# Stores issued from ScalarE's queue, attention outputs of two heads in turn, and three more cache buffers

## The chip, the cores and the metric

One NeuronCore of one Trainium2 chip runs the whole kernel. The metric is device time in microseconds of one execution, taken as the median of several runs.

The engines that matter here are TensorE (PE: matmuls, and PEld for its weight loads), VectorE (DVE), ScalarE (ACT), GpSimd (POOL) and SyncE (SP). SP only issues DMAs here. Each engine takes its instructions in the order in which the program lists them, and a DMA is one instruction on the engine that issues it.

## What is computed

The kernel runs one layer of a streaming encoder for 1024 prompt frames (8 tiles of 128) and 128 decode frames (8 requests of 16; a ninth tile, number 8). The reference, cut to the parts that this change touches:

```python
qa, ka, va, fl, qb, kb, vb, ga, gb = split(rms_norm(h, g_mix) @ w_in)   # 8 + 8 heads of 64
log_f = log_sigmoid(fl + b_f)
# outputs beside y: normalised ka, va, log_f of every frame, kb, vb of the newest 512 frames and the decode frames
s = q @ k.T * 64**-0.5 + bias        # mixer A: forget sums, causal; mixer B: relative bias, own chunk + 8 before
y = softmax(s) @ v                   # decode: keys/values are the cache (2048 rows A, 512 rows B) and the new ones
h += (sigmoid(ga) * (ya @ w_up_a) + sigmoid(gb) * (yb @ w_up_b)) @ w_out
h += peer_ffn(rms_norm(h))           # 8 heads x top-16 of 128*128 experts: rows of u and v per frame
h += sigmoid(rms_norm(h) @ w_ple_gate) * (p @ w_ple_proj)
```

## The kernel before

**Two groups of tiles.** Group 0 holds the decode tile and prompt tiles 0 to 2, group 1 the prompt tiles 3 to 7. By the profile's time the stages are: norm and attention of group 0 with the decode attention (0 to 510 us; "stage 0" below), its merge (510 to 715), its routing with the norm and first projections of group 1 ("route 0", 715 to 905), attention of group 1 ("attention 1", 905 to 1390), merge (1390 to 1710), routing ("route 1", 1710 to 2021), the expansion of group 1's expert weights into dense matrices G ("expand", 2021 to 2305), the dense expert pass (2305 to 3925) and the per-layer embedding (3925 to 4084).

**Attention** goes by units: a unit is two heads of one mixer, 64 columns each, side by side in one 128-wide tile. `project` makes q, k, v of one unit and tile, stores k and v to the outputs (L328, L329) and, in group 0, also the transposed keys and the values to the DRAM scratch `kT_d`, `v_d` (L350, L351), from which group 1 reads them back. `prompt` works one tile of one unit: for each of its two heads the scores `N`, the softmax `p`, transposes of `p` into `pt` (L494), an evacuation to SBUF as `pT` by ACT (`evac`, L80), and the output matmuls `po` (L497), whose two heads fill PSUM partitions 0 to 63 and 64 to 127, that is columns 0 to 63 and 64 to 127 of the array. Its score matmul for mixer A adds the forget sums with a selector `sel_p`.

**Decode** (group 0 only) streams the cache: keys `kcd` (L522) and values `vcd` (L586) come in pieces of 128 x 512 (256 KB) through one ring of `KC` buffers. A phase of four requests loads 16 key pieces (mixer A), makes the scores `Sd` (L547), the softmax, the transposes, and then the outputs `pod` (L591). These use four column groups of 32 in turn, one request in each. The code is interleaved: a unit's projections alternate with the attention of the unit before.

**Expert rows.** Group 0's experts are fetched row by row: an indirect DMA from POOL (L813) into a ring of 4, then one DVE instruction (L816 for u, L818 for v). There are 1,024 of these steps. They have low priority: a scheduler lays the first `G0` = 400 of them between the instructions of group 1 up to expand, by its own estimate of when each engine is free. Group 1's expand builds G (`ga`, `pg`, `stage`, L919 to L929) and stores it in 10 pieces of 4 MB (`G_d`, L933); some hidden units are worked out ahead and stored as `ge_d` (L968).

**Queues.** All loads and all stores are issued from SP, except the gathers. DMAs of SP and ACT take the semaphores DMAHW0 to DMAHW7 in turn, and an issue waits until the DMA that had the same semaphore before it has landed.

Of the kernel before, what the change touches and what calls it, by code (L numbers as in the profile page):

```python
# [8 lines left out]
F32 = mybir.dt.float32  # L9
F32R = mybir.dt.float32r  # L10
# [8 lines left out]
P = 128  # L19
# [7 lines left out]
PRE = tuple(range(3, 128, 4)) + tuple(range(1, 128, 32))  # L27
KC = 15
NP = 4
# [17 lines left out]
def build(tc, I, O, dbg=None, stop=None):  # L47
# [46 lines left out]
    m_blk = [const.tile([P, P], BF, name=f"m_blk{s}") for s in range(2)]  # L94
    sel_p = const.tile([P, 8, P], F32R, name="sel_p")
    qn = const.tile([P, 2], F32, name="qn")
# [33 lines left out]
    def setup_masks(dec):  # L130
# [18 lines left out]
        for s in range(2):  # L149
# [12 lines left out]
            nc.vector.tensor_copy(m_new[s], a)  # L162
        for q in range(2):
            t1 = tmp(f"t1{q}").rearrange("p (h c) -> p h c", h=4)
            t2 = tmp(f"t2{q}").rearrange("p (h c) -> p h c", h=4)

            o3 = one.rearrange("p (h c) -> p h c", h=4)
            for t, off in ((t1, 4 * q), (t2, 32 + 4 * q)):
                keep(t, o3, [[-1, 4], [0, P]], 0.0, -off, 1)
                keep(t, t, [[1, 4], [0, P]], 0.0, off, -1)  # L170
            nc.vector.tensor_tensor(sel_p[:, 4 * q:4 * q + 4, :], t1, t2, op=OP.add)
        for q in range(2):
# [87 lines left out]
    def attention_phase(g, tiles, aT, yT):  # L260
# [17 lines left out]
        def load_unit(u):  # L278
# [12 lines left out]
            if br == 1:  # L291
                Dn = at.tile([P, 2, 256], F32, tag="Dn", name=f"Dn{g}{u}")
                nc.sync.dma_start(Dn, I["biasP"][u - 4])
                for h in range(2):
                    hh = 2 * (u - 4) + h
                    nc.vector.tensor_scalar(Dn[:, h, :], Dn[:, h, :], rb0[:, hh:hh + 1], -1.0,
                                            op0=OP.subtract, op1=OP.mult)
                    nc.vector.memset(Dn[0:64, h, 192:256], BIG)
            return ws, kT, vU, Dn

        def project(u, n, t, ws, kT, vU, Dn):
# [25 lines left out]
            if ko is not None:  # L327
                nc.sync.dma_start(ko[rows, cu * P:(cu + 1) * P], kq[:, 0:P])  # L328
                nc.sync.dma_start(vo[rows, cu * P:(cu + 1) * P], vt)  # L329
            tp = bank(f"tp{nm}")  # L330
            nc.tensor.transpose(tp[:, 0:P], kq[:, 0:P], ident)
            nc.tensor.transpose(tp[:, P:2 * P], kq[:, P:2 * P], ident)
            qp = at.tile([P, 2, P], F32, tag="qp", name=f"qp{nm}", bufs=2 * nts if g == 0 else nts + 1)
            nc.gpsimd.memset(qp, 0.0)
            if t == TS:
                kTs = at.tile([P, P], F32, tag="kTs", name=f"kTs{nm}")
                nc.scalar.copy(kTs, tp[:, 0:P])
                q4 = qp.rearrange("p a c -> p (a c)").rearrange("p (b h i) -> p b h i", b=8, h=2)
                for h in range(2):
                    s = slice(64 * h, 64 * h + 64)  # L340
                    nc.scalar.activation(q4[s, :, h, :], tp[s, P:2 * P].rearrange("p (b i) -> p b i", i=16),
                                         AF.Copy, scale=qn[s, br:br + 1])
                pending.append(decode(u, br, qp, kTs, vU[:, slot[TS], :], n, at, dec, yT))
            else:
                nc.scalar.copy(kT[:, t * P:(t + 1) * P], tp[:, 0:P])
                for h in range(2):
                    s = slice(64 * h, 64 * h + 64)
                    nc.scalar.activation(qp[s, h, :], tp[s, P:2 * P], AF.Copy, scale=qn[s, br:br + 1])
                if g < len(GROUPS) - 1:
                    nc.sync.dma_start(kT_d[u, :, t * P:(t + 1) * P], kT[:, t * P:(t + 1) * P])  # L350
                    nc.sync.dma_start(v_d[u, :, t, :], vt)  # L351
                pending.append([lambda: prompt(g, u, br, t, n, qp, kT, vU, Dn, at, yT)])
# [27 lines left out]
    def logf(g, tiles, fl, at, dec):  # L380
# [31 lines left out]
        for i, t in enumerate(tiles):  # L412
            nc.sync.dma_start(O["lf"][:, t * P:(t + 1) * P], lT[0:8, i, :])
        pt = [t for t in tiles if t != TS]
# [37 lines left out]
    def prompt(g, u, br, t, n, qp, kT, vU, Dn, at, yT):  # L452
# [3 lines left out]
        W = nk * P  # L456
        po = bank(f"po{nm}")
        both = W <= 512 and wide[0] == 1024
        for h in range(2):
# [3 lines left out]
            for c0 in range(0, W, 512):  # L463
# [3 lines left out]
                if br == 0:  # L467
                    nc.tensor.matmul(N[:, c0:c1], qp[:, h, :], rhs, start=True, stop=False)
                    nc.tensor.matmul(N[:, c0:c1], sel_p[:, 2 * u + h, :], cP[:, c0:c1], start=False, stop=not last)
                    if last:  # L470
# [19 lines left out]
            for j0 in range(0, nk, 4):  # L490
# [4 lines left out]
                evac(pT[:, j0:j1, :], ps[:, 0:(j1 - j0) * P].rearrange("p (j c) -> p j c", c=P))  # L495
            for j in range(nk):
                nc.tensor.matmul(po[64 * h:64 * h + 64, 0:P], vU[:, k0 + j, 64 * h:64 * h + 64], pT[:, j, :],  # L497
                                 start=j == 0, stop=j == nk - 1)
        nc.scalar.copy(yT[:, u, n * P:(n + 1) * P], po[:, 0:P])
# [385 lines left out]
    def expand_phase():  # L885
# [21 lines left out]
        for n, t in enumerate(DT):  # L907
            rb, gT = ready
            for c0 in range(0, P, W):
# [22 lines left out]
                if c0 % 64 == 64 - W:  # L932
                    nc.sync.dma_start(G_d[2 * n + c0 // 64], stage)  # L933
        st.close()
# [28 lines left out]
    def hidden_phase(dn, n2h, n2l):  # L963
        with tc.high_priority(offset=FILL):
            for q, j in enumerate(PRE):
                ge = dn.tile([P, TD], F32, tag="ge", name=f"gp{j}")
                hidden(dn, ge, j, n2h, n2l, nc.gpsimd, True)
                nc.sync.dma_start(ge_d[q], ge)  # L968

# [221 lines left out]
```

## Time and profile before

| | us |
|---|---|
| three runs | 4101.39, 4101.27, 4084.70 |
| median | 4101.27 |
| the profiled execution | 4085.47 |
| its span, first to last instruction | 4083.8 |
| PE, DVE, ACT, POOL busy in it | 3716.3, 2969.9, 1539.4, 1721.3 |

The profiled execution is at the lower of the two levels of the three runs. The granted TensorE clock over the span is 0.964 of full speed. PE is busy for 91% of the span, but not in each stage for the same reason, so the profile has to be read by stages: busy time of each engine in the stage, then the waits of the busiest, then the mean of one instruction times its count.

### The profile page before, as it was taken

The page shows a single profiled execution, that of the slowest core. Times are in us where ns is not written, and L with a number is a line of the kernel's source. Part 1 is how long each engine was busy: PE and PEld are TensorE (multiplying, and loading weights), DVE is VectorE, ACT ScalarE, POOL GpSimd, SP SyncE. Part 2 cuts the span into 40 slices and gives each one's busy share as a digit, 9 for nine tenths or more (in the row PEclk, how much of TensorE's full clock was granted, in tenths as well). Part 3 has the DMA queues.
Part 4 walks back from the last instruction along what each step waited for, and adds up shares of the span by engine and source line. Part 5 has one row for each costly group of instructions (what it writes and reads, how often), then busy time and mean ns, then how long its engine had stood idle before and what let it go on. Part 6 is the DMA issues. An engine that isn't in the chain of part 4 may idle for free.

```text
span 4083.8 us, 57125 instructions
## 1 busy us (share of the span) xinstructions
PE 3716.3 (91%) x20520; PEld 3048.3 (75%) x20520; DVE 2969.9 (73%) x5571; ACT 1539.4 (38%) x3307; POOL 1721.3 (42%) x1360
## 2 busy tenths in 40 slices
PE   7988899869889897899897899999999999999999
PEld 6555566657767565798886788888888888888876
DVE  5122112899888777799888588888888888888862
ACT  5445412346565411224599722222222222212231
POOL 5112032137767555652310044555555555555520
PEclk8999999879999898899999999999999999999999
DMA  6777733328888898972343589989988998988952
GB/s 206 237 235 208 223 93 124 101 82 268 281 288 275 286 321 294 328 247 88 108 184 165 230 297 314 325 309 315 325 304 304 313 331 316 327 298 311 313 173 71
DMA packets 415116, 1002.49 MB, mean 245 GB/s; under 512 B 38816, under 2 KB 170352, under 8 KB 412400
## 3 DMA queue, kind: packets, MB, share of 16 engines
q0 software_dynamic: 147456, 536.94, 38.0%
q1 hardware_dynamic: 267376, 461.90, 34.0%
q8 instruction: 161, 2.64, 0.3%
q14 instruction: 123, 1.01, 0.1%
HBM read 917.19 MB, written 81.50 MB: 245 GB/s over the span
## 4 chain that ended last, share of the span: by engine, by line
issue 25%; PE 22%; DMA 20%; DVE 19%; POOL 11%; ACT 3%; SPq 0%; POOLq 0%; DVEq 0%; ACTq 0%
DMA v<-in_pv,gi 9%; POOL u L813 6%; DMA u<-in_pu,gi 5%; POOL v L813 4%; DVE gya L818 3%; DVE u L816 3%; PE Sd L547 2%; DMA vs<-in_pv 1%; DMA vcd<-in_vA 1%; PE z L209 1%; PE pu L638 1%; PE hd L958 1%; PE po L497 1%; PE z L210 1%; PE z L211 1%
## 5 line engine op out<-in xcount | busy, mean ns | idle before, releaser
L813 POOL DMA_INDIRECT v<-in_pv,gi x512 | 669.5, 1308 | 794.0 <-DVE gya L818 654.9
L813 POOL DMA_INDIRECT u<-in_pu,gi x512 | 669.2, 1307 | 494.3 <-DVE u L816 374.4
L816 DVE SCALAR_TENSOR_TENSOR u<-u,gn 128x1024 f32<-128x1024 f32 x512 | 630.0, 1239 | 167.0 <-DMA u<-in_pu,gi 164.5
L818 DVE SCALAR_TENSOR_TENSOR gya<-v,hid,gya 128x1024 f32<-128x1024 f32 x512 | 661.1, 1291 | 121.3 <-DMA v<-in_pv,gi 117.4
L1009 PE MATMUL py<-vh,wh 128*128 128x512 f32 x1280 | 507.9, 398 | 46.4 <-DVE yacc L1012 23.0
L1011 PE MATMUL py<-vh,wl 128*128 128x512 f32 x1280 | 497.9, 394 | 6.4 <-DVE wl L941 6.4
L1010 PE MATMUL py<-vl,wh 128*128 128x512 f32 x1280 | 502.4, 394 | 0.2 <-DVE vl L941 0.2
L958 PE MATMUL hd<-aTh,uh 128*128 128x320 f32 x2048 | 483.4, 313 | 21.0 <-ACT gp L961 14.1
L958 PE MATMUL hd<-aTh,ul 128*128 128x320 f32 x2048 | 482.8, 313 | 7.0 <-DVE ul L941 5.7
L958 PE MATMUL hd<-aTl,uh 128*128 128x320 f32 x2048 | 482.0, 313 | 0.0
L958 PEld LDWEIGHTS hd<-aTh,uh 128*128 128x128 f32 x2048 | 351.8, 191 | 31.9 <-ACT gp L961 16.0
L958 PEld LDWEIGHTS hd<-aTh,ul 128*128 128x128 f32 x2048 | 349.9, 190 | 13.7 <-DVE ul L941 7.8
L958 PEld LDWEIGHTS hd<-aTl,uh 128*128 128x128 f32 x2048 | 351.1, 191 | 4.0
L940 ACT CAST vh<-vs 128x1024 fp32r<-128x1024 f32 x128 | 134.1, 1052 | 500.0 <-DMA vs<-in_pv 267.7
L1009 PEld LDWEIGHTS py<-vh,wh 128*128 128x128 f32 x1280 | 242.4, 190 | 106.9 <-DVE yacc L1012 29.4
L1011 PEld LDWEIGHTS py<-vh,wl 128*128 128x128 f32 x1280 | 242.4, 189 | 61.3 <-DVE wl L941 10.6
L1010 PEld LDWEIGHTS py<-vl,wh 128*128 128x128 f32 x1280 | 242.8, 190 | 47.5 <-DVE vl L941 0.4
L940 ACT CAST uh<-us 128x1024 fp32r<-128x1024 f32 x128 | 134.2, 1048 | 285.7 <-PE hd L958 266.7
L940 ACT CAST wh<-ge 128x640 fp32r<-128x640 f32 x128 | 91.9, 727 | 390.7 <-DVE ge L987 195.5
L927 PE MATMUL pg<-obb,ga 128*128 128x128 f32 x1280 | 192.5, 296 | 42.2 <-ACT ga L923 22.2
L927 PEld LDWEIGHTS pg<-obb,ga 128*128 128x128 f32 x1280 | 164.0, 195 | 70.5 <-ACT ga L923 28.8
L1012 DVE TENSOR_TENSOR yacc<-yacc,py 128x1024 f32<-128x1024 f32 x160 | 192.4, 1214 | 11.5 <-PE py L1011 11.5
(1051 smaller groups left out, 7368.7 us busy)
## 6 DMA issues: line engine op xcount, KB each, us to landing
us<-in_uT SPq DMA_DIRECT2D x128, 512.0 KB
vs<-in_pv SPq DMA_DIRECT2D x128, 512.0 KB
G_d<-stage SPq DMA_DIRECT2D x10, 4096.0 KB
gj<-G_d SPq DMA_DIRECT2D x64, 640.0 KB
kcd<-in_kA SPq DMA_DIRECT2D x128, 256.0 KB
vcd<-in_vA SPq DMA_DIRECT2D x128, 256.0 KB
ge_d<-gp SPq DMA_DIRECT2D x36, 320.0 KB
ge<-ge_d SPq DMA_DIRECT2D x36, 320.0 KB
```

What stands on the lines that cost most here:

```text
L209: nc.tensor.matmul(out, lh[:, k, :], wh[:, a:b], start=first and k == 0, stop=False)
L547: nc.tensor.matmul(ps[32 * b4:32 * b4 + 32, :], q3[:, 4 * s + b4, :], rhs, start=br == 1 and q < nch, stop=True)
L813: nc.gpsimd.indirect_dma_start(out=r, out_offset=None, in_=I["pu" if k < P else "pv"], in_offset=bass.IndirectOffsetOnAxis(ap=gi[:, kk:kk ...
L816: nc.vector.scalar_tensor_tensor(r, r, 1.0, n2, op0=OP.mult, op1=OP.mult, accum_out=hid[:, kk:kk + 1])
L818: nc.vector.scalar_tensor_tensor(ya, r, hid[:, kk:kk + 1], ya, op0=OP.mult, op1=OP.add)
L927: nc.tensor.matmul(pg[:, c * P:(c + 1) * P], ga[:, b0 + c, :], ob[:, b0 + c, :], start=True, stop=True)
L940: nc.scalar.copy(out_h, src)
L958: nc.tensor.matmul(ps[sp][:, 0:Nw], a[:, k, :], b[:, k, sp * Nw:(sp + 1) * Nw], start=k == 0 and q == 0, stop=k == 7 and q == 2)
L1009: nc.tensor.matmul(py[:, c], wh[:, ns], vh[:, c], start=a, stop=False)
L1010: nc.tensor.matmul(py[:, c], wh[:, ns], vl[:, c], start=False, stop=False)
L1011: nc.tensor.matmul(py[:, c], wl[:, ns], vh[:, c], start=False, stop=z)
L1012: nc.vector.tensor_tensor(yacc[n], yacc[n], py, op=OP.add)
```

## The change

Three things change.

1. The stores of keys, values, log forgets, `kT_d`, `v_d`, `G_d` and `ge_d` are issued with `nc.scalar.dma_start` in place of `nc.sync.dma_start`, 215 DMAs in all (56 + 56 of values and keys, 24 + 24 to the scratch, 9 of log forgets, 10 of `G_d`, 36 of `ge_d`). A key store stands now behind the copy of the transposed keys.
2. In `prompt` both heads' `pT` are made first. Then `po` is allocated, and its matmuls alternate between the two heads, and so between the two column halves.
3. The selector `sel_p` shrinks from 8 x 128 to 8 columns (a broadcast supplies the rest), `qp` of group 0 has 6 buffers in place of 8, `Dn` one in place of two, and the cache ring `KC` 18 in place of 15.

```diff
-KC = 15
+KC = 18
...
-    sel_p = const.tile([P, 8, P], F32R, name="sel_p")
+    sel_p = const.tile([P, 8], F32R, name="sel_p")
...
-                Dn = at.tile([P, 2, 256], F32, tag="Dn", name=f"Dn{g}{u}")
+                Dn = at.tile([P, 2, 256], F32, tag="Dn", name=f"Dn{g}{u}", bufs=1)
...
             if ko is not None:
-                nc.sync.dma_start(ko[rows, cu * P:(cu + 1) * P], kq[:, 0:P])
-                nc.sync.dma_start(vo[rows, cu * P:(cu + 1) * P], vt)
+                nc.scalar.dma_start(vo[rows, cu * P:(cu + 1) * P], vt)
...
-            qp = at.tile([P, 2, P], F32, tag="qp", name=f"qp{nm}", bufs=2 * nts if g == 0 else nts + 1)
+            qp = at.tile([P, 2, P], F32, tag="qp", name=f"qp{nm}", bufs=nts + 2 if g == 0 else nts + 1)
...
                 nc.scalar.copy(kTs, tp[:, 0:P])
+                nc.scalar.dma_start(ko[rows, cu * P:(cu + 1) * P], kq[:, 0:P])
...
                 nc.scalar.copy(kT[:, t * P:(t + 1) * P], tp[:, 0:P])
+                if ko is not None:
+                    nc.scalar.dma_start(ko[rows, cu * P:(cu + 1) * P], kq[:, 0:P])
...
-                    nc.sync.dma_start(kT_d[u, :, t * P:(t + 1) * P], kT[:, t * P:(t + 1) * P])
-                    nc.sync.dma_start(v_d[u, :, t, :], vt)
+                    nc.scalar.dma_start(kT_d[u, :, t * P:(t + 1) * P], kT[:, t * P:(t + 1) * P])
+                    nc.scalar.dma_start(v_d[u, :, t, :], vt)
...
-            nc.sync.dma_start(O["lf"][:, t * P:(t + 1) * P], lT[0:8, i, :])
+            nc.scalar.dma_start(O["lf"][:, t * P:(t + 1) * P], lT[0:8, i, :])
...
-        po = bank(f"po{nm}")
+        pTs = []
...
-                    nc.tensor.matmul(N[:, c0:c1], sel_p[:, 2 * u + h, :], cP[:, c0:c1], start=False, stop=not last)
+                    nc.tensor.matmul(N[:, c0:c1], sel_p[:, 2 * u + h:2 * u + h + 1].broadcast_to([P, P]), cP[:, c0:c1], start=False, stop=not last)
...
-            for j in range(nk):
-                nc.tensor.matmul(po[64 * h:64 * h + 64, 0:P], vU[:, k0 + j, 64 * h:64 * h + 64], pT[:, j, :],
-                                 start=j == 0, stop=j == nk - 1)
+            pTs.append(pT)
+        po = bank(f"po{nm}")
+        for j in range(nk):
+            for h, pT in enumerate(pTs):
+                r = slice(64 * h, 64 * h + 64)
+                nc.tensor.matmul(po[r, 0:P], vU[:, k0 + j, r], pT[:, j, :], start=j == 0, stop=j == nk - 1)
...
-                    nc.sync.dma_start(G_d[2 * n + c0 // 64], stage)
+                    nc.scalar.dma_start(G_d[2 * n + c0 // 64], stage)
...
-                nc.sync.dma_start(ge_d[q], ge)
+                nc.scalar.dma_start(ge_d[q], ge)
```

**On TensorE, attention 1**, one pair of heads with 7 key tiles, before:

```order
L494 MATMUL pt_10859<-ident,p_10853 128x128 x4
L494 MATMUL pt_10865<-ident,p_10853 128x128 x3
L497 MATMUL po_10844<-pT_10858,vU_9920 64x128 x7
L494 MATMUL pt_10891<-ident,p_10885 128x128 x4
L474 MATMUL N_11103<-kT_10483,qp_10533 128x512
L494 MATMUL pt_10897<-ident,p_10885 128x128 x3
L497 MATMUL po_10844<-pT_10890,vU_9920 64x128 x7
```

and now (`po` is L501 there):

```order
L494 MATMUL pt_10876<-ident,p_10870 128x128 x4
L494 MATMUL pt_10882<-ident,p_10870 128x128 x3
L474 MATMUL N_11095<-kT_10476,qp_10526 128x512
L501 MATMUL po_10887<-pT_10850,vU_9913 64x128
L501 MATMUL po_10887<-pT_10875,vU_9913 64x128
```

Twelve more rows follow that repeat the last two. The two runs of seven have become one run of fourteen that alternates between the two `pT`, and no `pt` transposes stand between them any more.

**On SP, stage 0**, before, a key store stands among the loads of cache keys, with the waits in brackets:

```order
L522 DMA kcd_1223<-in_kA 128x512 [waits DMAHW1_49,PE_49]
L522 DMA kcd_1225<-in_kA 128x512 [waits DMAHW2_49,PE_49]
L328 DMA out_kA<-kq_1184 128x128 [waits DMAHW3_49,DVE_49,Activation_49]
L522 DMA kcd_1227<-in_kA 128x512 [waits DMAHW4_49,PE_49]
L522 DMA kcd_1229<-in_kA 128x512 [waits DMAHW5_49,PE_49]
L522 DMA kcd_1231<-in_kA 128x512 [waits DMAHW6_49,DMAHW2_49,PE_49]
L522 DMA kcd_1233<-in_kA 128x512 [waits DMAHW7_49,PE_49]
```

Now SP has loads alone, here at a later unit:

```order
L525 DMA kcd_4459<-in_kA 128x512 [waits DMAHW3_49,PE_49]
L525 DMA kcd_4461<-in_kA 128x512 [waits DMAHW4_49,PE_49]
L525 DMA kcd_4463<-in_kA 128x512 [waits DMAHW5_49,PE_49]
L525 DMA kcd_4465<-in_kA 128x512 [waits DMAHW6_49,PE_49]
L525 DMA kcd_4467<-in_kA 128x512 [waits DMAHW7_49,PE_49]
L525 DMA kcd_4469<-in_kA 128x512 [waits DMAHW0_49,PE_49]
L525 DMA kcd_4471<-in_kA 128x512 [waits DMAHW1_49,PE_49]
```

and ACT has the stores of that unit among its own work:

```order
L316 COPY vU_3919<-z_4111 128x128 [waits DVE_49]
L449 ACTIVATE p_4164<-p_4164,sm_4165 128x256 [waits DVE_49]
L345 DMA out_kA<-kq_4136 128x128 [waits DMAHW4_49,DVE_49]
L326 DMA out_vA<-vU_3919 128x128 [waits DMAHW6_49,Activation_49]
L351 DMA v_d<-vU_3919 128x128 [waits DMAHW0_49]
L502 COPY yT_253<-po_4075 128x128 [waits PE_49]
L447 ACTIVATE p_4178,sm_4179<-N_4174,mn_4176 128x256 [waits DVE_49]
L310 ACTIVATE kq_4264,ssz_4265<-z_4239 128x64 x4
L343 COPY kT_3918<-tp_4149 128x128 [waits PE_49]
```

The stores have moved from ahead of cache loads to ahead of ACT's copies. The semaphores that the three stores wait for (4, 6, 0) are those of three of the loads.

**On DVE, route 1**, from the last split of a weight (`wq17l`) on, where `tops`, `topi`, `sc` belong to the routing of group 1, and `gya` and `u` are expert rows of group 0; before:

```order
L701 TENSOR_TENSOR wq17l<-wq17s,wq17h 128x1024
L731 MAX tops_14841<-sc_15080 128x8 x2
L728 MAX tops_14838<-sc_15167 128x8 x2
L729 MAX_INDEX topi_14847<-tops_14842,sc_15094 128x8 x2
L821 TENSOR_TENSOR hid_8592<-hid_8592,gg_7593 128x128
L732 MAX_INDEX topi_14846<-tops_14841,sc_15080 128x8 x2
L729 MAX_INDEX topi_14843<-tops_14838,sc_15167 128x8 x2
L730 MATCH_REPLACE sc_15094<-tops_14842,sc_15094 128x128 x2
L818 SCALAR_TENSOR_TENSOR gya_8590<-v_0_8979,hid_8592,gya_8590 128x1024
```

and now (L819 is L816 of before, and L821 is L818):

```order
L704 TENSOR_TENSOR wq17l<-wq17s,wq17h 128x1024
L731 MAX tops_14831<-sc_15160 128x8 x2
L734 MAX tops_14834<-sc_15073 128x8 x2
L732 MAX_INDEX topi_14840<-tops_14835,sc_15087 128x8
L819 SCALAR_TENSOR_TENSOR u_113_8925,hid_8585<-u_113_8925,gn_8581 128x1024
L732 MAX_INDEX topi_14840<-tops_14835,sc_15087 128x8
L819 SCALAR_TENSOR_TENSOR u_114_8928,hid_8585<-u_114_8928,gn_8581 128x1024
L732 MAX_INDEX topi_14836<-tops_14831,sc_15160 128x8 x2
L819 SCALAR_TENSOR_TENSOR u_115_8931,hid_8585<-u_115_8931,gn_8581 128x1024
```

Here 16 expert-row steps stood between `wq17l` and the first `oa` of expand, and 31 stand there now. Ahead of the last attention instruction on DVE stood 219 of the 400, and now 206. Between this and `wq17l` the count is nearly as before.

## Rows read from the trace of the kernel before

**Rows 1.** Windows by stage: busy time (instructions) of each engine, TensorE clock, DMA share, GB/s.

```profile
core 0: us, PE busy (x) PEld busy (x) DVE busy (x) ACT busy (x) POOL busy (x), PEclk, DMA share, GB/s
0.00:510.00 510.00, 439.06 (x3406) 292.84 (x3406) 145.49 (x392) 253.07 (x838) 117.03 (x154) 0.94 0.74 222
...
905.00:1390.00 485.00, 432.27 (x2494) 335.64 (x2492) 414.19 (x783) 295.71 (x839) 344.18 (x294) 0.97 0.84 277
1390.00:1710.00 320.00, 273.66 (x1014) 192.99 (x1015) 242.91 (x341) 58.17 (x80) 185.87 (x145) 0.90 0.89 316
1710.00:2021.00 311.00, 286.87 (x1806) 276.95 (x1805) 294.28 (x1251) 111.84 (x193) 120.31 (x71) 0.96 0.50 166
2021.00:2305.00 284.00, 241.40 (x1632) 212.85 (x1630) 229.67 (x195) 283.25 (x502) 18.98 (x6) 0.98 0.39 159
2305.00:3925.00 1620.00, 1557.84 (x8256) 1378.14 (x8256) 1375.53 (x1517) 379.54 (x537) 835.31 (x621) 0.99 0.90 312
```

**Rows 2.** Groups of instructions, stage 0 (0:510): busy, mean ns, idle before and its releaser.

```profile
L591 PE MATMUL pod<-vcd,pTd 128*32 128x128 f32 x1280 | 54.1, 290 | 27.9 <-DMA vcd<-in_vA 26.6 <-ACT pTd L80 1.1
...
L497 PE MATMUL po<-pT,vU 128*64 128x128 f32 x192 | 33.2, 298 | 8.2 <-ACT pT L80 7.6
```

**Rows 3.** The same view, attention 1 (905:1390).

```profile
L816 DVE SCALAR_TENSOR_TENSOR u<-u,gn 128x1024 f32<-128x1024 f32 x128 | 160.9, 1262 | 28.0 <-DMA u<-in_pu,gi 27.2 <-DVE kq125r L216 0.4 <-issue 0.2
...
L497 PE MATMUL po<-pT,vU 128*64 128x128 f32 x856 | 118.1, 287 | 26.5 <-ACT pT L80 25.2 <-issue 1.2
...
L818 DVE SCALAR_TENSOR_TENSOR gya<-v,hid,gya 128x1024 f32<-128x1024 f32 x96 | 123.1, 1282 | 29.9 <-DMA v<-in_pv,gi 29.1 <-DVE gya L818 0.2 <-issue 0.2
```

**Rows 4.** Timeline of TensorE, 1113.5:1118: start, length, instruction and how many merged.

```profile
1114.34 1.09 PE L497 MATMUL po<-pT,vU 128*64 128x128 f32 x8
```

**Rows 5.** The chain that ended last, 0:510: start, length, what.

```profile
99.36 3.96 DMA kcd<-in_kA
...
155.28 1.29 PE pod L591 x34
157.11 9.32 DMA vcd<-in_vA
```

**Rows 6.** DVE's waits in attention 1 (905:1390): total, times, longest.

```profile
DVE gya L818 <- DMA v<-in_pv,gi: 29.1, 36, 2.1
DVE u L816 <- DMA u<-in_pu,gi: 27.2, 37, 2.0
```

**Rows 7.** Groups of instructions, route 1 (1710:2021).

```profile
L816 DVE SCALAR_TENSOR_TENSOR u<-u,gn 128x1024 f32<-128x1024 f32 x23 | 30.6, 1334 | 6.2 <-DMA u<-in_pu,gi 6.2
...
L818 DVE SCALAR_TENSOR_TENSOR gya<-v,hid,gya 128x1024 f32<-128x1024 f32 x16 | 25.2, 1573 | 0.0
```

**Rows 8.** Waits of SyncE's queue, stage 0 (0:510).

```profile
SPq L522 <- PE Sd L547: 50.6, 45, 5.0
...
SPq L328 <- DVE kq L316: 22.5, 10, 6.1
SPq L351 <- ACT vU L318: 13.8, 8, 4.0
SPq L350 <- ACT kT L345: 13.8, 12, 2.4
SPq L329 <- ACT vU L318: 13.1, 10, 2.0
...
SPq L586 <- DMA vcd<-in_vA: 9.9, 14, 1.7
```

**Rows 9.** TensorE's waits, stage 0 (0:510).

```profile
PE pod L591 <- DMA vcd<-in_vA: 26.6, 26, 2.5
PE z L209 <- ACT vU L318: 13.8, 3, 10.0
...
PE po L497 <- ACT pT L80: 7.6, 7, 1.4
PE ydd L596 <- ACT obd L594: 3.1, 6, 0.8
```

**Rows 10.** Issue of one line's DMAs: ns min/median/max, first and last start us.

```profile
L329 SPq DMA_DIRECT2D out_vA<-vU x16: 332/364/422, 64.6 to 400.7; - x16
```

**Rows 11.** Groups of instructions, expand (2021:2305).

```profile
L929 ACT COPY stage<-pg 128x512 f32<-128x512 f32 x158 | 151.9, 1153 | 0.7 <-PE pg L927 0.7
```

More of the change, by code (lines that the diff above doesn't have):

```diff
@@ L162, in setup_masks @@
             nc.vector.tensor_copy(m_new[s], a)
[L163 to L171, printed above, removed]
+        t1 = tmp("t1")[:, 0:8]
+        t2 = tmp("t2")[:, 0:8]
+        for t, off in ((t1, 0), (t2, 32)):
+            keep(t, one[:, 0:8], [[-1, 8]], 0.0, -off, 1)
+            keep(t, t, [[1, 8]], 0.0, off, -1)
+        nc.vector.tensor_tensor(sel_p, t1, t2, op=OP.add)
         for q in range(2):
```

## The prediction

> **What bounds the kernel now.** I read the table by stages first, then in each stage the waits of the engine that is busiest, and last the length of one instruction of each kind that the change touches. The stages have different limits [rows 1]. In stage 0 TensorE works 439 of 510 us and ScalarE only 253, so TensorE and what it waits for set the end. In attention 1 TensorE works 432 of 485 and VectorE 414, and VectorE also waits 29.1 + 27.2 = 56 us for expert rows to land [rows 6]: 414 + 56 = 470 of 485, so the row of expert-row steps is as near to the limit as TensorE is. There are 128 + 96 = 224 of these steps [rows 3], one each 485 / 224 = 2.17 us. In route 1 VectorE works 294 of 311, in expand ScalarE works 283 of 284, and in the dense pass TensorE works 1558 of 1620. The change adds nothing to the dense pass and takes nothing from it, so I leave it and the embedding at what they are.
>
> **Output matmuls on the two halves.** Before, eight `po` of one head start within 1.09 us less the last one's 0.29, so one each 0.11 us [rows 3, 4]. All eight use the same 64 columns. The nearest row with column groups in turn is the decode's `pod`, four groups of 32: 34 of them take 1.29 us, one each 0.03 us [rows 2, 5], though each moves 128 elements as `po` does. Four groups thus give nearly a factor of four, and two should give a factor of two: one `po` each 0.055 us. The saving of TensorE's time is 192 x 0.055 = 10 us in stage 0 [rows 2] and 856 x 0.055 = 47 us in attention 1 [rows 3]. The bounds are 0 and these. I take them whole as TensorE's time, since `pod` is the same form of instruction; what the stages make of it comes next.
>
> On this the Trainium skill ("TensorE: Matmul & The Clock Gate", section "Part 3: Packing small matmuls — row/col tiling") says that a weight load overlaps matmuls in flight only where its row group differs. Both halves use all 128 rows, so by that rule the loads would still queue and the saving be near 0; this is the fourth case below. The rule doesn't agree with the row of `pod`, whose four groups use all rows as well.
>
> **Attention 1 and route 1.** TensorE's 47 us don't all reach the end of the stage, since the expert rows pace it as well. The scheduler has put 206 of them ahead of the last attention instruction where 219 stood: 13 fewer, at 2.17 us, are 28 us. Between 0 (the stage is kept by something else) and 47 (TensorE alone sets it) I take 28, because VectorE was at 470 of 485. Its waits for projections and `pT` are small beside this. The 400 steps that precede expand are still 400. Merge 1 keeps its number, and route 1 gets 31 behind its last weight split where there were 16. In route 1 VectorE is the busy engine, and a step takes 1.33 us there [rows 7]: 15 x 1.33 = 20 us later into expand. The bounds are 3 (all of VectorE's 311 - 294 = 17 idle us taken up) and 15 x 1.57 = 24 [rows 7]. I take 20, since idle time there sits in front of results of TensorE and not where steps are. Attention 1 and route 1 together: -28 + 20 = -8, from -47 + 3 = -44 to +24.
>
> **Loads of the cache.** In stage 0 the stores' waits for data held up SP's queue 22.5 + 13.8 + 13.8 + 13.1 = 63 us [rows 8], and behind them stand the loads of keys and values. But SP waits as well for buffers, above all 50.6 us for `Sd` to release keys, and TensorE itself loses only 26.6 us to late values [rows 9]. Three more buffers let three more pieces be under way, and the lines of SP are free of stores. The gain lies between 0 and 26.6; pieces that TensorE waits for land 4 to 9 us after their issue [rows 5], and the longest wait is 2.5 us, so I take half, -13. The `qp` buffers, 8 to 6, and `Dn`, 2 to 1, cost nothing as long as `qp` is wanted for the tiles of one unit only; the expected cost is inside the bounds of the next term.
>
> On this the Trainium skill ("DMA: Bandwidth & Descriptors", section "Issuing engines are not separate DMA queues") says that all issuers share the same 16 engines, so that issuing from a second one saves the sequencer's issue time alone. By that rule the term would be 0 and the whole sum near -1. The rows show another thing that the move can save, the 63 us in which a store that waits for data stands ahead of loads; whether TensorE gets any of it no run here shows yet.
>
> **Stores on ScalarE.** 92 of the 215 stores fall into stage 0. One takes 0.33 to 0.36 us to issue [rows 10], so ScalarE gets 92 x 0.34 = 31 us of work. Beyond that a store waits for the DMA eight places earlier. In the order of the changed kernel that is, for some 70 of the 92, a load of SP. ScalarE then stands until that load has landed, and queued behind it are copies of `kT`, `vU`, `pT` and of `po`, for which TensorE waits. The nearest row is SP's own wait for the same thing, 9.9 us in 14 times, 0.7 each [rows 8]: 70 x 0.7 = 49 us. At the upper end half of a landing time of 4 us [rows 5] gives 70 x 2 = 140 us. How much of it reaches TensorE? Now 253 us of ScalarE's work [rows 1] cost TensorE 13.8 + 7.6 + 3.1 = 24.5 us of waits [rows 9], a tenth. A tenth of 31 + 49 to 31 + 140 is 8 to 17 us; I take +13. If it were a third of the upper end, it would be 57. In attention 1 some 77 stores add 77 x 0.34 = 26 us to ScalarE's 296 of 485; the loads ahead of them have long landed there, so a tenth of it, under 3 us, hides behind the pace of the expert rows. If that cover is gone it is the 3 us.
>
> **Expand.** ScalarE has no idle time there. Ten `G_d` issues are 10 x 0.36 = 3.6 us, and a few `ge_d` lie in it too: +4. If each issue also waits for the end of the copy before it, 1.15 us [rows 11], it is 4 + 11 = 15. That SP is relieved there brings nothing.
>
> **The sum.** Stage 0: -10 - 13 + 13 = -10. Attention 1 and route 1: -8. Expand: +4. Total -14 us on the profiled execution's 4085.5. That execution is at the lower of two levels of the three runs, 4085 and 4101. The median is at the upper one; I apply the sum to the median, 4101.3 - 14 = 4087.
>
> **The rivals.**
> - *B, the stages give TensorE's time back in full.* Attention 1 shrinks by 45 of its 47 us, because VectorE's 56 us of waits shrink too; route 1 takes up half of the moved steps in idle time, +10; of the late values 20 us vanish, and the stores cost stage 0 only +5, since ScalarE is idle for half of it. With -10 for `po` and +4 in expand that is -10 - 20 + 5 - 45 + 10 + 4 = -56: 4045. For it: both engines of attention 1 would fit into 440 us, TensorE with 385 and VectorE with 414 less 13 x 1.27. Against it: the pace of the expert rows would have to fall below 2.1 us.
> - *C, ScalarE's waits lengthen the decode.* A third of 171 us reaches TensorE, +57 in place of +13: the sum is +30, 4131. For it: ScalarE's copies stand right behind the stores in the order. Against it: ScalarE waits for TensorE much of the time, so some of the standing replaces a wait. It decides from the point at which stage 0 loses more than 13 + 14 = 27 us to it.
> - *D, the halves don't overlap* (the change doesn't do what it says). The -10 is gone. In attention 1 TensorE has its 432 us still, and of the 28 only half is left, while route 1 gets its 20: -13 + 13 - 14 + 20 + 4 = +10, 4111. Against it: `pod`.
>
> **How the numbers follow.** About 0.5%, 20 us, is what a measurement of this kernel can tell from no change: below 4081 is faster, above 4122 slower. The forecast of -14 has a chance of 0.41, B 0.34, C 0.17, D 0.08. Of the forecast's 0.41 some 0.08 fall below -20 and 0.02 above +20; of B 0.30 are faster; of C 0.15 slower; of D nearly all is the same. Faster: 0.08 + 0.30 = 0.38. Slower: 0.02 + 0.15 + 0.01 = 0.18. Same: 0.44. The range reaches to B's time and somewhat beyond, 4040, and to C's, 4132. The likeliest case alone has 4065 to 4105.
>
> **What would show it.** Right: rows of `po` in the timeline with fourteen in 0.055 x 13 + 0.29 = 1.0 us; attention 1 at some 457 us; the wait for late values near 13; ScalarE waiting for DMA in stage 0 for 50 to 140 us with TensorE's waits for ScalarE up by about 13; route 1 at some 331 us; expand at 288. Wrong: `po` still one each 0.11 us (D); TensorE's waits for ScalarE in stage 0 above 27 us more than now (C); attention 1 below 445 us and route 1 below 320 (B).

## The result and the profile after

The changed kernel takes 4047.67 us (median of 4 runs, 4043.39 to 4051.47) against 4097.16 (median of 4, 4084.70 to 4101.39): a ratio of 0.9884 with a 95% interval of 0.9858 to 0.9910, so faster by 49 us or 1.2%. The kernel before spread from 4079 to 4112 us over some 60 executions, with no gap of more than 5 us, so the two levels of its first three runs were chance. The forecast of 4087 missed the size. The time lies in the range of 4040 to 4132, 3 us from the time of rival B. The profiled execution took 4043.39 us, with a span of 4041.4; it is 42 us below the profiled execution of before, so the traces account for 42 of the 49 us.

The stages of the changed kernel, with the columns of [rows 1]: stage 0 to the last decode output, attention 1 from the first expert row on, merge 1, route 1, expand, dense.

```profile
0.00:468.00 468.00, 412.00 (x3404) 283.62 (x3404) 140.98 (x391) 250.25 (x835) 111.59 (x149) 0.97 0.80 240
857.00:1334.00 477.00, 402.53 (x2527) 307.96 (x2526) 405.62 (x797) 295.65 (x846) 324.22 (x286) 0.93 0.83 269
1334.00:1712.00 378.00, 330.98 (x1418) 249.72 (x1415) 299.31 (x513) 77.36 (x114) 221.73 (x170) 0.93 0.89 313
1712.00:1975.00 263.00, 235.57 (x1468) 227.54 (x1467) 255.66 (x1087) 93.73 (x156) 105.97 (x61) 0.95 0.50 160
1975.00:2269.00 294.00, 242.10 (x1591) 213.32 (x1590) 231.83 (x201) 286.81 (x506) 15.20 (x5) 0.96 0.37 152
2269.00:3880.00 1611.00, 1552.64 (x8237) 1377.27 (x8235) 1376.14 (x1517) 376.61 (x534) 840.47 (x621) 0.99 0.90 313
```

To compare stages of kernels whose times have shifted, I read the same landmarks in each timeline: the last decode output, the first expert-row gather, the last output matmul of attention 1, the last weight split (`wq17l`), the first `oa` of expand, and the first and last matmul of the dense pass's output (`py`). In us from the start of the span, with the kernels of the experiments below:

| kernel | decode end | 1st gather | attention 1 end | `wq17l` | 1st `oa` | 1st `py` | last `py` | end |
|---|---|---|---|---|---|---|---|---|
| before | 508.0 | 898.1 | 1389.8 | 1774.0 | 2010.8 | 2328.7 | 3924.5 | 4083.8 |
| changed | 468.0 | 857.4 | 1334.2 | 1712.3 | 1975.4 | 2289.5 | 3879.8 | 4041.4 |
| stores only | 505.7 | 893.7 | 1402.8 | 1779.3 | 2014.8 | 2333.6 | 3927.3 | 4086.3 |
| ring only | 476.3 | 863.9 | 1347.6 | 1731.0 | 1973.7 | 2291.6 | 3906.9 | 4068.5 |
| halves only | 515.9 | 905.8 | 1367.3 | 1744.8 | 2014.8 | 2324.9 | 3924.6 | 4084.7 |
| stores and ring | 468.9 | 854.8 | 1367.3 | 1751.8 | 1985.0 | 2305.6 | 3902.1 | 4062.5 |
| ring and halves | 468.6 | 858.9 | 1328.1 | 1703.3 | 1966.1 | 2277.9 | 3874.1 | 4034.0 |
| changed, 15 buffers | 503.7 | 892.2 | 1375.4 | 1754.0 | 2008.3 | 2325.7 | 3926.8 | 4086.5 |
| changed, 20 buffers | 458.3 | 847.5 | 1329.7 | 1715.6 | 1967.7 | 2287.3 | 3895.5 | 4053.5 |
| ring of 20 and halves | 455.6 | 848.0 | 1315.1 | 1698.7 | 1961.5 | 2271.3 | 3877.7 | 4037.7 |

By the first two lines stage 0 gained 40 us and attention 1 (gather to last output matmul) 491.7 - 476.8 = 15; merge 1 gained 6, and route 1 lost 263.1 - 236.8 = 26. Expand (first `oa` to first `py`) and the dense pass gained 4 and 6, and the tail lost 2.

The three kinds of matmul that the change reaches in stage 0, in the view of [rows 2] over 0:468 of the changed kernel:

```profile
L550 PE MATMUL Sd<-kcd,qp 128*32 128x512 f32 x320 | 90.0, 603 | 1.2 <-DMA kcd<-in_kA 0.8 <-DMA kcd<-in_kB 0.4
L594 PE MATMUL pod<-vcd,pTd 128*32 128x128 f32 x1280 | 43.9, 274 | 8.5 <-DMA vcd<-in_vA 6.1 <-ACT pTd L80 2.0
...
L501 PE MATMUL po<-pT,vU 128*64 128x128 f32 x192 | 28.3, 325 | 15.4 <-ACT pT L80 15.3
```

`pod` went from 54.1 busy and 27.9 idle ahead of it to 43.9 and 8.5 [rows 2], which is 30 us. The waits for values are 6.1 of 26.6 us [rows 9]. `po` won 5 us busy and lost 8 in waits for `pT`. The key matmuls `Sd` were no term of the prediction; the view of before over 0:508 has for them

```profile
L547 PE MATMUL Sd<-kcd,qp 128*32 128x512 f32 x320 | 100.3, 617 | 1.2 <-DVE Nd L557 0.6 <-DMA kcd<-in_kA 0.6
```

so another 10 us went there, in busy time and not in waits. These busy times also hold a difference in TensorE's granted clock, 0.97 in stage 0 now against 0.94 [rows 1].

The alternating outputs in the changed kernel's timeline of TensorE (1000:1016; start, length, instruction), and the row of attention 1 (857:1334):

```profile
1002.44 1.09 PE L501 MATMUL po<-pT,vU 128*64 128x128 f32 x14
...
1014.31 1.31 PE L501 MATMUL po<-pT,vU 128*64 128x128 f32 x20
```

```profile
L819 DVE SCALAR_TENSOR_TENSOR u<-u,gn 128x1024 f32<-128x1024 f32 x128 | 159.1, 1244 | 28.9 <-DMA u<-in_pu,gi 28.4 <-DVE sm L448 0.2
L821 DVE SCALAR_TENSOR_TENSOR gya<-v,hid,gya 128x1024 f32<-128x1024 f32 x83 | 106.2, 1279 | 26.3 <-DMA v<-in_pv,gi 25.7 <-DVE sm L448 0.3
L501 PE MATMUL po<-pT,vU 128*64 128x128 f32 x864 | 63.0, 285 | 13.4 <-ACT pT L80 13.3
```

These rows count records, and a matmul is two of them here. Twenty records take 1.31 us, (1.31 - 0.29) / 19 = 0.054 us each, where one took 0.11 [rows 4]; the fourteen of the first row take 0.062 each. Their busy time in attention 1 is 63.0 instead of 118.1 us [rows 3]. TensorE's whole busy time from the first gather to the last output matmul fell by less, from 439 to 402 us, at a granted clock of 0.93 in place of 0.97. VectorE still waits 54 us there for expert rows, as in [rows 6].

### The profile page after: what moved, and what is told of

Its sections match the earlier page's. It is cut to its first block, busy times and chain, and to the rows that moved or that the text cites. A ratio compares the mean times of both kernels' runs of the same rounds, so it can differ in the third digit from the quotient of the medians.

```text
span 4041.4 us, 57050 instructions
## 1 busy us (share of the span) xinstructions
PE 3653.6 (90%) x20520; PEld 3013.1 (75%) x20520; DVE 2970.8 (74%) x5570; ACT 1535.4 (38%) x3307; POOL 1717.0 (42%) x1356
## 4 chain that ended last, share of the span: by engine, by line
issue 25%; DMA 21%; DVE 20%; PE 20%; POOL 11%; ACT 2%; POOLq 0%; SPq 0%; DVEq 0%; ACTq 0%
DMA v<-in_pv,gi 10%; POOL u L816 6%; DMA u<-in_pu,gi 5%; POOL v L816 4%; DVE u L819 4%; DVE gya L821 3%; PE Sd L550 2%; DMA vs<-in_pv 2%; PE hd L961 1%; PE pu L641 1%; PE z L207 1%; PE z L208 1%; PE z L209 1%; DVE topi L735 1%; DVE sc L733 1%
## 5 line engine op out<-in xcount | busy, mean ns | idle before, releaser
L816 POOL DMA_INDIRECT v<-in_pv,gi x512 | 667.2, 1303 | 828.1 <-DVE gya L821 678.3
L816 POOL DMA_INDIRECT u<-in_pu,gi x512 | 668.2, 1305 | 500.3 <-DVE u L819 360.3
L819 DVE SCALAR_TENSOR_TENSOR u<-u,gn 128x1024 f32<-128x1024 f32 x512 | 637.1, 1252 | 157.3 <-DMA u<-in_pu,gi 155.0
L821 DVE SCALAR_TENSOR_TENSOR gya<-v,hid,gya 128x1024 f32<-128x1024 f32 x512 | 662.6, 1294 | 119.4 <-DMA v<-in_pv,gi 114.9
L961 PEld LDWEIGHTS hd<-aTh,uh 128*128 128x128 f32 x2048 | 352.7, 191 | 27.3 <-ACT gp L964 14.7
L1012 PEld LDWEIGHTS py<-vh,wh 128*128 128x128 f32 x1280 | 242.7, 190 | 102.6 <-DVE yacc L1015 27.9
```

The costliest lines, as they stand in the source:

```text
L816: nc.gpsimd.indirect_dma_start(out=r, out_offset=None, in_=I["pu" if k < P else "pv"], in_offset=bass.IndirectOffsetOnAxis(ap=gi[:, kk:kk ...
L819: nc.vector.scalar_tensor_tensor(r, r, 1.0, n2, op0=OP.mult, op1=OP.mult, accum_out=hid[:, kk:kk + 1])
L821: nc.vector.scalar_tensor_tensor(ya, r, hid[:, kk:kk + 1], ya, op0=OP.mult, op1=OP.add)
L961: nc.tensor.matmul(ps[sp][:, 0:Nw], a[:, k, :], b[:, k, sp * Nw:(sp + 1) * Nw], start=k == 0 and q == 0, stop=k == 7 and q == 2)
L1012: nc.tensor.matmul(py[:, c], wh[:, ns], vh[:, c], start=a, stop=False)
```

## The experiments

Theories at the start: **Q** (stage 0 gained because the loads no longer stand behind stores), **R** (it gained by the three buffers), **H** (the alternating halves carry the gain). Ratios are to the kernel before, run on the same chip in the same session, with the 95% interval.

**Part 1 alone.** Edit: the lines of the diff with `nc.scalar.dma_start`, nothing else.

> The kernel before with part 1 alone: the 215 stores issued from ScalarE's queue; one output run per head and 15 cache buffers as before. Theory Q (the queue): stage 0 lost 40 us because SP's loads no longer stand behind stores that wait for data, so this alone gives most of it, -25 to -35 us in stage 0, TensorE's wait for late values from 26.6 to under 12 us. Theory R (the ring): the three more buffers did it, so this gives -5 to -10 in stage 0 and the wait for values stays above 18 us. Both: expert-row steps ahead of the end of attention 1 are 222 as against 219, so no gain there, and the total is the stage's gain within 10 us. If ScalarE's waits for loads cost what the prediction feared, stage 0 is above 508 us.

Measured: 4098.19 us, ratio 1.0010 (0.9995 to 1.0025). Decode ends at 505.7, the wait for values is 15.1 us, but `po`'s wait for `pT` rose from 7.6 to 13.4. Stage 0 gained 2 us, which is less than either theory said, and 15.1 lies between their bounds. Q falls as the main cause: TensorE exchanged one wait for another. Nor did the stores lengthen stage 0. Attention 1 took 509.1 us instead of 491.7, though only 3 expert-row steps more stood in it.

**Part 3 alone.**

```diff
-KC = 15
+KC = 18
...
-    sel_p = const.tile([P, 8, P], F32R, name="sel_p")
+    sel_p = const.tile([P, 8], F32R, name="sel_p")
```

(and the making and use of `sel_p`, `qp` and `Dn` as in the change)

> The kernel before with part 3 alone: 18 cache buffers, the small selector, 6 qp buffers, one Dn; stores stay on SP's queue. Theory R: -25 to -35 us in stage 0 and the wait for late values under 12 us. Theory Q: -5 to -10 us, the wait above 18 us. Attention 1 has 215 steps as against 219: -4 there and about +5 in route 1.

Measured: 4058.39 us, ratio 0.9910 (0.9887 to 0.9932). Decode ends at 476.3, 32 us earlier, so R holds, though the wait for values is at 14.7 and not under 12 us. SP's wait for `Sd` to release a key buffer, 50.6 us before [rows 8], is less than half of it here (0:476):

```profile
SPq L520 <- PE Sd L545: 20.4, 23, 2.6
```

The same view as above, over 0:476 of this kernel, shows where the rest came from:

```profile
L545 PE MATMUL Sd<-kcd,qp 128*32 128x512 f32 x320 | 86.3, 628 | 1.8 <-DMA kcd<-in_kA 1.8
...
L589 PE MATMUL pod<-vcd,pTd 128*32 128x128 f32 x1280 | 47.8, 279 | 15.9 <-DMA vcd<-in_vA 14.7 <-ACT pTd L80 1.2
```

`Sd` fell by 14.0 us busy, and `pod` by 6.3 busy and 12.0 idle: 32 together. `Sd` waited for hardly any key before either. What changed is how its matmuls stand in the program: as I read it, the scheduler puts a key matmul where it expects the key. A run is a row of key matmuls with no other matmul between them. In the order of the kernel before, the 160 key matmuls stand in 82 runs, 43 of them of a single one; with the ring alone in 66 runs, 23 single. The timeline of before has both kinds (105:125 and 181:190; each matmul is two records):

```profile
108.32 1.06 PE L547 MATMUL Sd<-kcd,qp 128*32 128x512 f32 x8
...
181.79 1.04 PE L547 MATMUL Sd<-kcd,qp 128*32 128x512 f32 x2
```

Four matmuls on the four column groups take 1.06 us, and one alone takes 1.04. A run thus costs about 1 us in most cases, however many of its four places are filled (one run of four in the same window took 1.90): 82 - 66 = 16 runs fewer at some 1 us, against 14.0 us measured. The traces of all fourteen kernels agree: in the order in which the key matmuls end, the four with the fewest runs (60 to 67) have 76 to 86 us of `Sd`, the five with the most (83 to 91) have 99 to 106.

**Part 2 alone.** Edit: the two hunks of the diff in `prompt` on `pTs` and `po`.

> The kernel before with part 2 alone: output matmuls of two heads in turn. Theory Q and R alike: one output matmul each 0.055 us, the busy time of the outputs in attention 1 from 118 to about 63 us, stage 0 within 5 us of 508; 201 expert-row steps ahead of the end of attention 1 where 219 stood, so attention 1 -15 to -25 us, and 36 steps in route 1 where 16 stood, so route 1 +20 to +30: total between -5 and +10. The rival (theory H: the halves carry the gain): -25 or more in total.

Measured: 4084.37 us, ratio 0.9969 (0.9954 to 0.9985), 12 us less by the medians, more than the 5 expected at most. The outputs do what was expected (65.8 us busy in attention 1), and attention 1 is 461.5 us, 30 shorter. Route 1 gives that back, with 20 more steps behind `wq17l` than before: it takes 270.0 instead of 236.8 us. The rows of route 1 in this kernel (1745:2015):

```profile
L819 DVE SCALAR_TENSOR_TENSOR u<-u,gn 128x1024 f32<-128x1024 f32 x20 | 29.6, 1481 | 3.2 <-DMA u<-in_pu,gi 3.2
L821 DVE SCALAR_TENSOR_TENSOR gya<-v,hid,gya 128x1024 f32<-128x1024 f32 x16 | 27.7, 1734 | 0.0
```

29.6 + 3.2 us of the 33 are the moved steps. The first `oa` comes 4 us later than before, after 8 lost in stage 0, where `Sd` rose from 100.3 to 106.4 us. The profiled execution is no shorter than that of before (spans of 4084.7 and 4083.8), so the traces don't show where the 12 us come from. H falls as the main cause.

**Parts 1 and 3.** Edit: both of the above, `prompt` as before.

> Parts 1 and 3 together, without the alternating outputs. If the gain of the whole change is that of the loads in stage 0, this is at 4045 to 4060 us, -35 to -50, and attention 1 and route 1 are as in the kernel before (222 steps, 14 behind the last weight split). If the halves carry the gain it is above 4080.

Measured: 4063.16 us, ratio 0.9924 (0.9898 to 0.9950), some 3 us above what was expected for a gain from the loads. Decode ends at 468.9, 7 us earlier than with the ring alone, and the wait for values is 0.5 us. But attention 1, expected as before, takes 512.5 us against 483.7 with the ring alone and 491.7 before. This was the second sign that the stores cost something in attention 1.

**The buffers back to 15, and to 16.** A second pair of theories: **M**, a threshold (15 buffers can't hold the 16 keys of a phase), and **N**, depth (each buffer lets one more piece be under way).

```diff
-KC = 18
+KC = 15
```

> The changed kernel with 15 cache buffers again; the small selector, 6 qp buffers, one Dn, the stores on ScalarE and the alternating outputs stay. It separates the ring from what was given up for it. If the three buffers are the cause: the last decode output ends at 500 to 510 us as before (468 in the changed kernel, 508 before), the total at 4075 to 4090. If the small selector or the fewer qp buffers did it: below 480 and the total as the changed kernel's.

Measured: 4084.85 us, ratio 0.9966 (0.9949 to 0.9983), decode end 503.7. The buffers are the cause, not what was given up for them.

```diff
-KC = 18
+KC = 16
```

> The changed kernel with 16 cache buffers. A phase loads 16 key pieces, request by request, but uses them quarter by quarter over all four requests, so the 13th must land before the first is freed. Theory M (a threshold): 15 buffers can't hold the 16 keys of a phase, 16 can, so the first added buffer gives most of the gain, the last decode output at 475 to 482 us. Theory N (depth): each buffer lets 256 KB more be under way and gives a third, so it is at 488 to 497.

Measured: 4077.75 us, ratio 0.9949 (0.9926 to 0.9971), decode end 492.9: 10.8 us for the first buffer and 24.9 for the next two. That is N, in what a buffer gives; how many pieces were under way at a time was not counted.

**Keys loaded in the order of use**, 15 buffers in the kernel before:

```diff
-            for b4 in range(4):
+            if br == 0:
+                kc = [[None] * 4 for _ in range(4)]
+                for q in range(4):
+                    for b4 in range(4):
+                        kt = dec.tile([P, 512], F32, tag="kc", name=f"kc{nm}{b4}{q}", bufs=KC)
+                        nc.sync.dma_start(kt, I["kA"][4 * s + b4, uu, :, q * 512:(q + 1) * 512])
+                        kc[b4][q] = kt
+            for b4 in range(4 if br == 1 else 0):
                 b = 4 * s + b4
-                if br == 0:
-                    parts = []
-                    for q in range(4):
...
```

> The kernel before with one change: a phase's key loads are issued quarter by quarter over the four requests, as they are used, not request by request. 15 buffers, stores on SP. Theory M: the ring is freed in the order in which it is filled, four buffers after four pieces instead of after 13, so most of the gain comes without a buffer, the last decode output at 470 to 485 us and TensorE's wait for late values under 15 us. Theory N: no more bytes are under way at a time, 500 to 510 us and over 22 us of that wait.

Measured: 4089.38 us, ratio 0.9981 (0.9962 to 0.9999), decode end 500.7, wait for values 24.0 us. M falls again: the order in which the ring is freed is worth 7 us of stage 0 at most.

The same edit on the changed kernel:

> The changed kernel with the key loads quarter by quarter as well. Theory M: with 18 buffers a part of the same limit is left, so a further -5 to -15 us, the last decode output at 453 to 463 us. Theory N: within 4 us of the changed kernel's 468.

Measured: 4058.87 us, ratio 0.9913 (0.9881 to 0.9944), decode end 473.7, so nothing gained, if anything 6 us lost. M's range is missed, and N's by 2 us.

**Fewer expert rows ahead of expand.**

```diff
-G0 = 400
+G0 = 384
```

> The changed kernel with G0 = 384 in place of 400: 16 expert-row steps fewer ahead of expand, so 15 stand behind the last weight split of route 1 where 31 do, and 640 are left for the dense pass, as many as it has places for. Theory G (the alternating outputs shorten attention 1, and route 1 gives it back by the steps that moved there): route 1 is 16 x 1.33 = 21 us shorter, the dense pass longer by 0 to 10, total -11 to -21 against the changed kernel. Rival (route 1 is kept by TensorE or by the routing's own chain): within 5 us of it.

Measured: 4060.40 us, ratio 0.9915 (0.9890 to 0.9941), 13 us above the changed kernel and not 11 to 21 below it; the two intervals overlap. Route 1 did what theory G said: `wq17l` to the first `oa` is 235.2 us instead of 263.1, and the first `py` comes at 2268.3, 21 us earlier. Then the dense pass took 1607 us instead of 1590, which is within what it varies between these traces (1590 to 1615), and the tail 183 instead of 162, where the other traces have 158 to 162, since the steps hadn't all found room:

```profile
3875.00:4057.00 182.00, 147.76 (x576) 106.14 (x576) 69.77 (x89) 37.82 (x60) 9.93 (x13) 0.89 0.32 109
```

```profile
L821 DVE SCALAR_TENSOR_TENSOR gya<-v,hid,gya 128x1024 f32<-128x1024 f32 x9 | 11.6, 1284 | 7.1 <-DMA v<-in_pv,gi 6.9
```

The first is the window of the tail (columns as in [rows 1]), the second its expert-row steps: nine are left, with 7 us of waits.

**Twenty buffers.**

```diff
-KC = 18
+KC = 20
...
-            qp = at.tile([P, 2, P], F32, tag="qp", name=f"qp{nm}", bufs=nts + 2 if g == 0 else nts + 1)
+            qp = at.tile([P, 2, P], F32, tag="qp", name=f"qp{nm}", bufs=nts + 1 if g == 0 else nts + 1)
```

> The changed kernel with 20 cache buffers, paid for by 5 qp buffers in place of 6. From 15 to 16 to 18 the last decode output went 504, 493, 468 us, some 12 us for each buffer. Theory N, straight on: 444 us, total 4020 to 4030. Theory N with an end (TensorE's wait for late values is 6 us now, so little is left to gain): 458 to 466. If a fifth qp buffer is too few: over 468.

Measured: 4046.25 us, ratio 0.9863 (0.9834 to 0.9892). Decode end 458.3: N, flattening to 5 us a buffer (with one `qp` buffer fewer). In the total it can't be told from the changed kernel.

**Parts 2 and 3, stores on SP.**

> Parts 2 and 3 without part 1: the stores stay on SP. With the ring alone stage 0 ended at 476 us, with ring and stores at 469, though the stores alone did nothing. If the stores' queue matters with a deep ring only: 474 to 480 here and the total 5 to 10 us above the changed kernel's. If the 7 us between those two were chance: within 3 us of 468 and of the changed kernel's total.

Measured: 4031.70 us (4029.43 to 4035.84), ratio 0.9833 (0.9810 to 0.9856). Both expectations missed: it isn't slower than the changed kernel but faster, by 16 us. Its interval ends where the other's begins; the two ran in different sessions, against befores of 4097.6 and 4097.2. Stage 0 ends at 468.6, as with the stores moved. The difference is behind it: from the first gather to the first `oa` 1107.2 us, against 1118.0 in the changed kernel.

Set against the ring alone, this run also shows that part 2 is worth more beside the ring than by itself: 0.9910 falls to 0.9833, 27 us by the medians (0.9924 to 0.9884 with the stores on ScalarE), where part 2 alone gave 0.9969. The traces have 8 us of it in stage 0, 3 from the first gather to the first `oa`, 6 in expand and 19 in the dense pass, in which the ring alone is the longest of all; why it is more is open.

The pairs that differ in part 1 alone show the same in attention 1 (in the third, the kernel with the stores on ScalarE also has the small selector, 6 `qp` buffers and one `Dn`; the last is the run with 20 buffers above and the one described below). TensorE's waits for ScalarE there, all lines added up, and the stretch from first gather to first `oa`:

| pair | stores on SP | stores on ScalarE | gather to `oa`, SP | ScalarE |
|---|---|---|---|---|
| kernel before | 50.8 | 62.1 | 1112.7 | 1121.1 |
| with ring | 47.7 | 62.3 | 1109.8 | 1130.2 |
| with halves | 61.0 | 76.6 | 1109.0 | 1116.1 |
| with both | 59.2 | 72.3 | 1107.2 | 1118.0 |
| with both, 20 buffers | 64.1 | 74.0 | 1113.4 | 1120.2 |

In every pair the waits rise by 10 to 16 us and the stretch by 7 to 20. A single difference of 7 in the stretch says little: with the keys in the order of use and the stores on SP it is 1118.4. And the total shows a cost beyond the intervals, just, in the fourth pair alone (0.9833 and 0.9884); the others are at 1 and 1.0010, 0.9910 and 0.9924, 0.9969 and 0.9966, 0.9858 and 0.9863. The waits themselves, in the second pair, first with the ring alone (864:1348) and then with the stores on ScalarE (855:1367):

```profile
PE po L495 <- ACT pT L80: 26.6, 29, 2.7
PE pt L492 <- ACT pT L80: 14.0, 12, 4.2
PE z L207 <- ACT vU L316: 4.1, 6, 1.8
```

```profile
PE po L497 <- ACT pT L80: 29.9, 31, 3.2
PE pt L494 <- ACT pT L80: 13.8, 10, 3.2
PE z L207 <- ACT vU L316: 9.3, 7, 3.4
PE pt L494 <- ACT p L449: 6.3, 4, 2.5
```

It is spread over the copies and the softmax that stand behind stores, a little in each.

The waits are not all of it. In this pair attention 1 is 29 us longer, and TensorE's busy time in it rises by 18 (columns as in [rows 1]; first with the ring alone, then with the stores on ScalarE):

```profile
863.90:1347.60 483.70, 433.58 (x2518) 333.36 (x2516) 414.44 (x801) 297.43 (x842) 342.66 (x296) 0.99 0.83 276
854.80:1367.30 512.50, 451.79 (x2531) 347.38 (x2531) 431.58 (x830) 301.44 (x850) 366.05 (x303) 0.95 0.81 267
```

The granted clock is 0.95 in place of 0.99. In the five pairs it is 0.97 and 0.96, 0.99 and 0.95, 0.94 and 0.92, 0.93 and 0.93, 0.94 and 0.92, lower with the stores on ScalarE in four of them. Whether the waits brought the clock down or it fell for another reason is not shown, so a part of the longer stretch may be the clock's.

**The best parts together**, 20 buffers, halves, stores on SP:

> Parts 2 and 3 with 20 cache buffers (5 qp buffers), stores on SP: the best of the parts put together. Theory N: TensorE still waited 17 us for late values with 18 buffers and the stores on SP, so two more buffers bring some 10 us in stage 0, the last decode output at 455 to 462 us (469 with 18), that wait under 10 us. Theory A (the stores on ScalarE cost attention 1 some 10 to 15 us through TensorE's waits for ScalarE): without them these waits in attention 1 are at 55 to 62 us here as in the kernels with the stores on SP, and not at 70 or more. Total 4018 to 4030.

Measured: 4039.39 us, ratio 0.9858 (0.9836 to 0.9879). Decode end 455.6, as expected, but with 13.1 us of waits for values and not under 10, and TensorE's waits for ScalarE in attention 1 are 64.1 us, between the two groups. The total missed its range and is not better than with 18: the first `py` comes 7 us earlier (2271.3), but the dense pass took 1606 us instead of 1596. Why is open. Nor is it better than the changed kernel with 20 buffers, which has the stores on ScalarE (0.9863). Parts 2 and 3 with 18 buffers have the lowest median here; the intervals of the two kernels with 20 overlap theirs.

## Why the prediction was right and wrong

The range held the time; the likeliest case did not (its own range was 4065 to 4105). Rival B gave the time, but not the reasons: B wanted 45 us from attention 1 and half of the moved steps absorbed by route 1, and neither happened. That its sum came within 3 us is luck: stage 0 gave 40 us where B had 25 and the forecast 10, and attention 1 with route 1 cost 11 where B had a gain of 35 and the forecast one of 8. Merge 1 and the dense pass, left at nothing, are 6 us shorter each; both vary by more than that between these traces.

- **The halves: right.** 0.054 us a record as forecast (the sign of fourteen in 1.0 us took records for matmuls: fourteen matmuls are 28 records), 55 us off the outputs' busy time in attention 1, and rival D is out. The rule of the Trainium skill that was weighed here ("TensorE: Matmul & The Clock Gate", section "Part 3: Packing small matmuls — row/col tiling"), that a weight load overlaps matmuls in flight only where the row group differs, does not agree with these rows: both halves use all rows.
- **Attention 1 and route 1: the mechanism was right, sizes were off.** Part 2 alone gave 30 us in attention 1 (28 forecast) and took 33 in route 1 (20 forecast); a step there took 1.48 us plus waits and not 1.33. In the whole change the pair came to -15 + 26 against -28 + 20. With the stores on SP it was -23 + 26 (ring and halves), so moving the stores took back 8 of the first.
- **Loads of the cache: the term that was mis-sized.** -13 was forecast; the ring alone gave -32. I counted only the waits for values and halved them. Two things were missed. SP's waits for buffers were weighed as if TensorE lost nothing by them, but from 15 to 18 buffers each gave 12 us. And late keys hid in the program's order: key matmuls set apart cost about 1 us each, which the view shows as busy time, not as a wait.
- **Stores on ScalarE, stage 0: right in kind.** ScalarE's waits for loads did appear. Those for `kcd` and `vcd` are 20.8 us (0:468), with the largest three

```profile
ACT pT L80 <- DMA vcd<-in_vA: 10.8, 4, 3.0
...
ACT yT L502 <- DMA kcd<-in_kA: 4.0, 1, 4.0
...
ACT vU L316 <- DMA kcd<-in_kA: 2.7, 1, 2.7
```

  and not 49 to 140: half a landing time for each of 70 was far too much. TensorE's waits for ScalarE in stage 0 rose from 33.4 us with the ring alone to 47.2 with ring and stores, about the 13 forecast; earlier values paid for it, 14.7 us of waits there against 0.5. In the other four pairs they rose by 6, 8, 6 and 21 us, and the waits for values fell by 10 to 13. Rival C is out. The second rule of the Trainium skill that was weighed ("DMA: Bandwidth & Descriptors", section "Issuing engines are not separate DMA queues"), that a second issuer saves issue time alone, agrees with the total of part 1 alone, 1.0010, though not because nothing moved: 11.5 us less wait for values stood against 6 more for `pT`.
- **Stores on ScalarE, attention 1: the step that failed.** The "under 3 us" that "hides behind the pace of the expert rows" was a tenth of 26 us of issue. It is 10 to 16 us of waits, and the stretch to expand is 7 to 20 longer, in part perhaps by the clock. As I read it, TensorE and ScalarE alternate there in short steps, so that the average of stage 0 was no measure for it.
- **Expand: about as forecast.** From first `oa` to first `py` the five pairs are 1, 3, 7, 2 and 10 us longer with the stores on ScalarE; +4 was forecast. That the whole change gained 4 us there is not the stores' doing, since the kernels with the halves and the stores on SP are at 310 to 312 us, against 318 before.

Part 1, then, moves the end of stage 0 by something between 12 us earlier and 3 later (1 earlier with ring and halves in place) and costs 7 to 20 us later. Beside the other two parts the kernel is 16 us better without it at 18 buffers; at 20 no difference in the total can be told. The waits point to ScalarE's queue as the way the cost takes; which of the stores does it was not tried.

## What to carry to other kernels

A wait list shows only the waits that leave an engine idle: where a scheduler places work by expected arrival, late data also shows as work that is spread thin, so count how an operation's instructions are grouped. Deepen the ring of a streamed input before moving stores about; where the stores move to an engine that another waits for, count how much those waits grow as well as what the loads save. When a stage gets shorter, look for what filled its gaps: those steps go somewhere, and in route 1, which was nearly full, they cost their whole length.

## What the runs showed of the hardware

- One key matmul on a group of 32 columns took 1.04 us alone, and a run of four took 1.06 (another run of four 1.90).
- Two column halves with the same rows took 0.054 to 0.062 us per record in turn, against 0.11 on one half. The nine kernels with the halves in turn have a granted clock of 0.92 to 0.94 in attention 1, the five without 0.95 to 0.99.
- The dense pass, with the same 8112 matmul records, took from 1590 to 1615 us in the profiled runs (1590 in the changed kernel, 1615 with the ring alone) at a clock of 0.99 in both; TensorE's waits in it were 57.6 and 74.3 us. Runs of one kernel differ by 6 to 29 us; whether this stage is where they do is not shown, since each kernel has one trace.
